# A down projection of seven quarter products by the Strassen-Winograd scheme, in a layer kernel whose order is planned

## The chip, the cores and the metric

One core of one Trainium2 chip. The metric is the device time of one execution in microseconds (us), as the median of several runs. A core has five engines that the text names: TensorE (PE; its weight loads, PEld, run beside the products), VectorE (DVE), ScalarE (ACT), GpSimd (POOL) and SyncE (SP), which here only issues transfers. They run side by side and wait for one another by semaphores. Products land in PSUM, of which the kernel has eight banks of 512 float32 columns on 128 partitions; everything else lies in SBUF.

## The reference

One layer of a diffusion backbone: 512 latent tokens and 256 context tokens of width 1024. A parallel attention and state-space mixer comes first, then a gated MLP. The change is in the last product of the MLP.

```python
D_MODEL, SEQ, D_FF, FFN_CONV = 1024, 512, 2816, 3

def conv_glu(h, w_up, conv_w, conv_b, w_down):
    gate, val = jnp.split(h @ w_up, 2, axis=-1)
    gate = depthwise_conv(gate, conv_w, conv_b)
    return (jax.nn.gelu(gate, approximate=False) * val) @ w_down
...
        ffn_x = conv_glu(modulate(rms_norm(x, ffn_pre_norm[l]), mod_x[3], mod_x[4]),
                         w_up[l], ffn_conv_w[l], ffn_conv_b[l], w_down[l])
        x = x + mod_x[5] * rms_norm(ffn_x, ffn_post_norm[l])
```

All arrays are float32.

## The kernel before

**Precision.** A product of float32 matrices is made of three products in the faster type F32R: `split` (L496 to 499) makes a high part by a copy on ACT (L498) and the rest, source minus high part, by a subtraction on DVE (L499). High times high, high times low and low times high are summed in PSUM. `weight` (L501) loads a block of weights and splits it; so each block of weights costs one transfer, one ACT copy and one DVE subtraction of its width.

**Stages, in order of time.** Input projections; state-space groups and attention, interleaved; the output projection (`natural_gemm`); the up projection; the down projection; the last norm and the output. The matmuls of the up projection are at L759 (in `gemm_T`, which several stages share), those of the down projection at L1519.

**Up.** For each of the 22 blocks j of 128 hidden columns, two blocks of weights, 1024 wide (`upw`), are multiplied with the normed tokens `h2`, into a pair of banks. That is 2 x 8 x 3 = 48 matmuls of 512 columns for a j. (The first three j, `EARLY`, go in two halves of 256 tokens.) `gated` (L1457) makes the convolution, the Gelu and the gate out of the two banks: one ACT operation (L1460), two DVE operations (L1461, L1463), ACT (L1465), DVE (L1466). The result, `gT[j]`, has 128 hidden columns on the partitions and 512 tokens in the row. `modblock(5, ...)` (L1300, its DVE operation at L587) and `modfinish` make the last gate row `g2` meanwhile.

**Down.** Two halves of 512 output columns, one after the other in the program, each with four banks, one for each 128 tokens. For each of 22 k, the half row of weights (256 KB) is loaded and split; in the first half `gT[k]` is split too (`parts`), and kept for the second. The last four k are kept back, and done one token block after another, so that a block is done early and its eviction lies beside the products of the next. The eviction takes the sum of squares on ACT (L1539) and multiplies with `g2` on DVE (L1540). When a token block has both halves, `last` (L1498) makes the norm's scale from the sums (L1503, L522 to 529), loads the rows held since the mixer, adds them (L1509), and stores.

**What sets the order.** Nothing above is executed in program order. The kernel is built twice: the first time to collect its instructions, then `plan` (L382) makes an order for each engine and a place for each buffer, and the second time the order is laid down by dependences. `price` (L162) gives a cost for each instruction; for a transfer it is a size divided by 360 (bytes by nanosecond), or `DMA_WORDS` for one that scatters words. `Graph.schedule` (L315) is a list scheduler over the five engines, which `best` runs forwards and backwards. SBUF is 212 units of 256 columns (`UNITS`), in blocks of four; a block holds one type at a time. `plan` gives each buffer a place that should be free by `MARGIN` (2500 ns) before the buffer's start in the last schedule, schedules again with the waits that the places bring, and repeats this `rounds` times. The round with the shortest time by these prices is used. `pins` are extra orders among matmuls: one kept group after another.

All loads and stores of the stages told of here are issued by SP, in one planned order. A transfer waits at the head of that queue until its buffer is free.

Of the kernel before, what the change touches and what calls it, by code (L numbers as in the profile page):

```python
# [11 lines left out]
F32 = mybir.dt.float32  # L12
# [138 lines left out]
AHEAD = 40000  # L151
DMA_START, DMA_WAIT, DMA_AHEAD, DMA_ALONE, DMA_WORDS = 650, 910, 3000, 0.8, 5000

# [8 lines left out]
def price(x):  # L162
# [6 lines left out]
    if "DMA" in kind:  # L169
        words = any(len(v.bass_ap.ap) > 1 and v.bass_ap.ap[-1][0] != 1 for v in x.outs if hasattr(v, "bass_ap"))  # L170
        return DMA_WORDS if words else size(ops[0]) * ops[0][1][0][1] * 4 / 360
    if e == "PE":
# [208 lines left out]

def plan(ins, pieces, hints, units, rounds=16):  # L382

# [20 lines left out]
    _, _, start, end = Graph(preds, eng, dma, cost, share, tables, urgent, opens, shared).best()  # L404
    found = None
    for _ in range(rounds):
        held, types = [(-1, -1e9, [])] * units, [None] * (units // 4)
        inst, before = [((), -1e9)] * (units // 4), [((), -1e9)] * (units // 4)
        full, places = [set(p) for p in preds], []
        for t, (n, type_), at in pieces:  # L410
# [10 lines left out]

            fit = [o for o in able if free[o] + MARGIN <= s0]
            fit = [o for o in fit if (o >= EDGE) == (n < 3)] or fit
# [20 lines left out]
        if found is None or took < found[0]:  # L444
            found = took, places, order
    return found
# [20 lines left out]
def build(nc, tc, ctx, a, out, dbg=None, places=None):  # L467
# [979 lines left out]

    gT = []
    EARLY = 3

    h2v = lambda k, p_: h2[k // 2 * 2 + p_][:, k % 2, :]
# [5 lines left out]
    def gated(j, gate, other, used):  # L1457

        cv = t2()
        act(cv, gate, AF.Identity, scale=R("fw", j * 3 + 1), bias=R("fb", j))  # L1460
        V.scalar_tensor_tensor(out=cv[:, 1:], in0=gate[:, : S - 1], scalar=R("fw", j * 3), in1=cv[:, 1:], op0=ALU.mult,  # L1461
                               op1=ALU.add)
        V.scalar_tensor_tensor(out=cv[:, : S - 1], in0=gate[:, 1:S], scalar=R("fw", j * 3 + 2), in1=cv[:, : S - 1],  # L1463
                               op0=ALU.mult, op1=ALU.add)
        act(cv, cv, AF.Gelu)  # L1465
        V.tensor_tensor(out=cv, in0=other, in1=cv, op=ALU.mult)  # L1466
        pfree(*used)
        gT.append(cv)


# [40 lines left out]

    lefts = {}
    for half in range(2):
        c0_ = half * 512
        po = [pget("a") for _ in range(NX)]

        def products(k, i, w, l):
            for lp, wp in ((0, 0), (0, 1), (1, 0)):
                mm(po[i], lhsT=l[lp][:, i * P : (i + 1) * P], rhs=w[wp], start=(k == 0 and lp == 0 and wp == 0),  # L1519
                   stop=(k == NF - 1 and lp == 1))  # L1520

        tail = []
        for k in range(NF):
            if not half:
                lefts[k] = parts(gT[k])
            w = weight(a["wdn"][k][:, c0_ : c0_ + 512], 512)
            if k < NF - 4:
                for i in range(NX):
                    products(k, i, w, lefts[k])
            else:  # L1530
                tail.append((k, w, lefts[k]))
        at = []
        for i in range(NX):
            began = here()
            for k, w, l in tail:
                products(k, i, w, l)
            at.append((began, here()))
            to = res[i][:, c0_ : c0_ + 512]
            act(t2(), po[i], AF.Square, accum_out=sums[i][:, half : half + 1])  # L1539
            V.tensor_tensor(out=to, in0=po[i], in1=g2[:, c0_ : c0_ + 512], op=ALU.mult)  # L1540
            pfree(po[i])
            if half:
                last(i, 2)
        pins.extend(zip(at, at[1:]))
    return sl.pieces, (pins, urgent, holds)

# [97 lines left out]
```

## Time and profile before

| what | us |
|---|---|
| median of 3 runs | 976.13 |
| lowest and highest | 975.1, 976.65 |
| the profiled execution | 976.79 |
| its span, from first to last instruction | 975.0 |

The profiled execution is one more execution; its span is 1.79 us shorter than its time, which also has what lies before the first and after the last instruction. The mean granted clock of TensorE in it is 0.995 of full speed.

The lines that follow in the prediction are of five kinds. The page's first part gives busy time, share and count of instructions of each engine; its second part cuts the span in 40 equal slices and gives tenths of busy time. A row of windows gives a stretch in us from the span's start, its length, then busy time and count for each engine, the granted clock, the share of the DMA engines and GB/s. A row of groups gives line, engine, operation, what is written and read, shapes, count, then busy time, mean ns of one, idle time of the engine before them and what ended it. A row of a line gives smallest, median and largest duration in ns and the first and last start. A row of the timeline, or of the chain of waits, gives start and length in us and what ran.

### The profile page before, as it was taken

To read this page: it belongs to the slowest core of one execution; us is meant where nothing else is said; L and a number is where in the kernel's file an instruction comes from. 1 tells how busy PE (TensorE), PEld (TensorE's weight loads), DVE (VectorE), ACT (ScalarE), POOL (GpSimd) and SP (SyncE) were. 2 spreads that over 40 slices of the span, in tenths; PEclk is the share of its full clock that TensorE was granted. 3 is DMA by queue.
4 is the path that set the end of the run, shared out by engine and by line. 5 is a ranking of instruction groups with operands and counts; after the bars stand their busy time and mean duration, and the time that the engine had idled before them with its cause. 6 is when DMAs were issued, how large, how long until landed. Compare 5 with 4: busy or idle time off the path is not lost.

```text
span 975.0 us, 14205 instructions
## 1 busy us (share of the span) xinstructions
PE 953.7 (98%) x5157; PEld 813.6 (83%) x5157; DVE 680.0 (70%) x1151; ACT 504.7 (52%) x1004; POOL 184.4 (19%) x187
## 2 busy tenths in 40 slices
PE   8999999999999999999899999999999999999997
PEld 7888888888878987888798888988888888878885
DVE  6999886999999987767789966735254342695214
ACT  4554337567579787787787026633142231662001
POOL 0002202657694535111010001000000000000000
PEclk9999999999999999999899999999999999999999
DMA  9924102012321351524839876231323203347321
GB/s 349 402 94 130 44 22 82 19 66 74 95 60 55 100 153 45 133 74 110 234 138 335 248 205 216 87 108 54 140 85 132 87 33 108 98 155 241 82 84 65
DMA packets 48037, 122.94 MB, mean 126 GB/s; under 512 B 8400, under 2 KB 11552, under 8 KB 47968
## 3 DMA queue, kind: packets, MB, share of 16 engines
q1 hardware_dynamic: 45424, 120.89, 38.6%
q10 hardware_dynamic: 2544, 1.15, 0.5%
q8 instruction: 41, 0.67, 0.3%
q14 instruction: 28, 0.23, 0.1%
HBM read 99.82 MB, written 6.46 MB: 109 GB/s over the span
## 4 chain that ended last, share of the span: by engine, by line
PE 80%; DVE 5%; DMA 3%; ACT 2%; issue 1%; POOL 0%; SPq 0%; DVEq 0%; ACTq 0%; POOLq 0%
PE banks L759 38%; PE banks L1519 12%; PE banks L1326 9%; PE banks L1203 5%; PE banks L1231 3%; PE banks L1219 3%; DVE block L499 2%; DMA block<-block 2%; PE banks L1135 1%; PE banks L686 1%; PE banks L1039 1%; PE banks L1084 1%; PE banks L1076 1%; DVE smalls L1205 1%; PE banks L808 1%
## 5 line engine op out<-in xcount | busy, mean ns | idle before, releaser
L759 PE MATMUL banks<-block,block 128*128 128x512 f32 (+1 forms) x2132 | 443.2, 360 | 1.1 <-DVE block L855 1.1
L759 PEld LDWEIGHTS banks<-block,block 128*128 128x128 f32 x2132 | 358.8, 188 | 62.1 <-DVE block L855 1.4
L499 DVE TENSOR_TENSOR block<-block,block 128x512 fp32r<-128x512 f32 (+4 forms) x252 | 221.7, 904 | 121.2 <-ACT block L498 59.2
L498 ACT ACTIVATE block<-block 128x512 fp32r<-128x512 f32 (+5 forms) x252 | 181.7, 746 | 220.6 <-PE banks L759 68.9
L1519 PE MATMUL banks<-block,block 128*128 128x512 f32 x504 | 118.1, 389 | 0.2 <-ACT block L498 0.2
L1519 PEld LDWEIGHTS banks<-block,block 128*128 128x128 f32 x504 | 94.4, 188 | 20.4 <-ACT block L498 0.8
L1203 PE MATMUL banks<-block,block 128*128 128x512 f32 (+1 forms) x384 | 97.8, 359 | 7.1 <-DMA block<-in_wout_dram 3.1
L522 POOL TENSOR_TENSOR smalls<-smalls,powers 128x1 f32<-128x1 f32 (+3 forms) x16 | 12.6, 789 | 482.5 <-DVE smalls L1503 355.4
L499 DVE TENSOR_TENSOR block<-banks,block 128x256 fp32r<-128x256 f32 (+1 forms) x156 | 84.1, 556 | 14.8 <-ACT block L498 13.8
L1326 PE MATMUL banks<-block,block 128*128 128x512 f32 x384 | 91.2, 393 | 0.0
L498 ACT ACTIVATE block<-banks 128x256 fp32r<-128x256 f32 (+1 forms) x156 | 74.8, 499 | 27.9 <-PE banks L1219 14.5
L1326 PEld LDWEIGHTS banks<-block,block 128*128 128x128 f32 x384 | 71.5, 188 | 14.3
L1203 PEld LDWEIGHTS banks<-block,block 128*128 128x128 f32 x384 | 61.0, 192 | 16.0 <-ACT block L1207 4.5
L1205 DVE TENSOR_REDUCE smalls<-banks 128x1 f32<-128x768 f32 x64 | 60.9, 951 | 17.5 <-PE banks L1203 13.8
L1231 PE MATMUL banks<-block,block 128*128 128x256 f32 x384 | 70.1, 297 | 0.0
L1207 ACT ACTIVATE block<-banks,smalls 128x768 f32<-128x768 f32 x64 | 57.9, 905 | 15.4 <-DVE smalls L1205 10.7
L1219 PE MATMUL banks<-cst,block 128*128 128x128 f32 x384 | 64.3, 275 | 0.2
L587 DVE SCALAR_TENSOR_TENSOR block<-block,block 128x1024 f32<-128x1024 f32 x50 | 60.0, 1217 | 3.8 <-DMA block<-in_wmod_dram 3.6
L1231 PEld LDWEIGHTS banks<-block,block 128*128 128x128 f32 x384 | 57.8, 191 | 4.5 <-issue 0.7
L793 DVE SCALAR_TENSOR_TENSOR block<-banks,cwh,block 128x510 f32<-128x510 f32 (+3 forms) x88 | 50.9, 619 | 8.1 <-ACT block L789 7.7
L1219 PEld LDWEIGHTS banks<-cst,block 128*128 128x128 f32 x384 | 47.3, 141 | 6.9 <-DVE block L499 0.8
L686 PE MATMUL banks<-block,block 128*128 128x512 f32 x192 | 48.3, 398 | 0.6 <-ACT block L640 0.6
(228 smaller groups left out, 980.1 us busy)
## 6 DMA issues: line engine op xcount, KB each, us to landing
block<-in_wmod_dram SPq DMA_DIRECT2D x48, 512.0 KB
block<-in_wup_dram SPq DMA_DIRECT2D x44, 512.0 KB
block<-in_wdn_dram SPq DMA_DIRECT2D x44, 256.0 KB
block<-block SPq DMA_DIRECT2D x32, 256.0 KB
block<-in_wout_dram SPq DMA_DIRECT2D x16, 512.0 KB
block<-block SPq DMA_DIRECT2D x56, 128.0 KB
block<-in_wxbc_dram SPq DMA_DIRECT2D x12, 512.0 KB
block<-in_wz_dram SPq DMA_DIRECT2D x16, 256.0 KB
```

Source lines behind the costliest of these rows:

```text
L498: act(hi, src, AF.Copy)
L499: (lo_eng or V).tensor_tensor(out=lo, in0=src, in1=hi, op=ALU.subtract)
L587: V.scalar_tensor_tensor(out=junk, in0=wt, scalar=0.5, in1=vec, op0=ALU.mult, op1=ALU.mult, accum_out=acc)
L686: mm(po[i], lhsT=hx[k][:, hp, i * P : (i + 1) * P], rhs=wz[wp], start=(k == 0 and wp == 0 and hp == 0), stop=(k == KD - 1 and hp == 1))
L759: mm(po, lhsT=wf(k, pt[0]), rhs=xf(k, pt[1]), start=(k == 0 and pt == parts[0]), stop=(k == nk - 1 and pt == parts[-1]))
L1203: mm(sc[:, o : o + n], lhsT=q_[:, x_, qi * P : (qi + 1) * P], rhs=kk[:, y_, :], start=part == 0, stop=part == 2)
L1205: V.reduce_max(nm, sc[:, :T], axis=AX.X, negate=True)
L1207: act(pe, sc[:, :T], AF.Exp, bias=nm, scale=1.0, accum_out=sm_)
L1219: nc.tensor.transpose((tx if c < NX else tc_)[:, o : o + P], pe[:, s_ : s_ + P], ident)
L1231: mm(po[:, half * 256 : half * 256 + 256], lhsT=vst(c), rhs=rhs, start=(part == 0 and c == 0), stop=(part == 1 and c == NKT - 1))
L1326: mm(po[i][:, nh * 512 : nh * 512 + 512], lhsT=l[lp][:, i * P : (i + 1) * P], rhs=w[wp][:, nh * 512 : nh * 512 + 512], start=(k == 0 and l ...
L1519: mm(po[i], lhsT=l[lp][:, i * P : (i + 1) * P], rhs=w[wp], start=(k == 0 and lp == 0 and wp == 0), stop=(k == NF - 1 and lp == 1))
```

## The change

The down projection is written as a product of two-by-two quarters. On the left, A is the activations: with tokens 0 to 255 and 256 to 511 as rows and hidden blocks 0 to 10 and 11 to 21 as columns, A11, A12 are the first tokens, A21, A22 the others. On the right, B has hidden blocks 0 to 10 and 11 to 21 as rows, and output columns 0 to 511 (`upper`) and 512 to 1023 (`lower`). In place of the eight quarter products there are seven, by Winograd's form of Strassen's scheme:

- sums of the left: A21 + A22, that minus A11, A11 - A21, and A12 minus the second (`mixed`). `combined` makes them on GpSimd in the up stage, four operations of 256 columns for each pair of hidden blocks (k, k + 11), as soon as block k + 11 is there. It also splits A11 and the first three sums, and keeps both parts of all four (`lefts[k]`, two buffers of 1024 columns).
- sums of the right: B12 - B11 (t1), B22 - t1 (t2_), B22 - B12 (t3), and B21 - t2_. They are made on DVE in the down stage.

The down stage is two series over the 11 pairs. Series 1 (`sums_of_right`) makes four products at once, two banks of 128 tokens for each: all eight banks. It loads a whole row of weights (512 KB) and half of another (256 KB), makes t1, t2_, t3, stores t2_ to DRAM, and splits B11, t2_, t3 and t1. Series 2 (`rest_of_right`) makes the other three, in six banks: it loads a whole row and t2_, makes B21 - t2_, splits it and both halves of the row, and splits `gT[11 + k]` and `mixed[k]`. A matmul is as before: 128x128 weights, 512 moving columns, three for each product of blocks. The last three (series 1) and four (series 2) pairs are kept back and done product by product. An eviction now adds a product to what was summed (`plus`), and where an output quarter is complete, `scaled` takes the squares on ACT and multiplies with `g2` on DVE.

Three things of the planner change: `DMA_WORDS` goes from 5000 to 10000; a transfer from SBUF to SBUF is priced at 180 in place of 360 bytes by nanosecond; and there are 56 rounds in place of 16, those from the tenth on with a margin drawn between 0 and 5000 ns, and every third of these starts again from the best schedule found.

```diff
@@ -149,7 +149,7 @@
          ("Pool", "Activation"): 75, ("Pool", "DVE"): 74, ("Pool", "PE"): 149, ("Pool", "Pool"): 102}
 
 AHEAD = 40000
-DMA_START, DMA_WAIT, DMA_AHEAD, DMA_ALONE, DMA_WORDS = 650, 910, 3000, 0.8, 5000
+DMA_START, DMA_WAIT, DMA_AHEAD, DMA_ALONE, DMA_WORDS = 650, 910, 3000, 0.8, 10000
 
 
 def engine_of(x):
@@ -168,7 +168,8 @@
     kind = type(x).__name__
     if "DMA" in kind:
         words = any(len(v.bass_ap.ap) > 1 and v.bass_ap.ap[-1][0] != 1 for v in x.outs if hasattr(v, "bass_ap"))
-        return DMA_WORDS if words else size(ops[0]) * ops[0][1][0][1] * 4 / 360
+        inside = all(isinstance(o[2].bass_ap.tensor, tile.Tile) for o in ops)
+        return DMA_WORDS if words else size(ops[0]) * ops[0][1][0][1] * 4 / (180 if inside else 360)
     if e == "PE":
         if ops[1][2].dtype == mybir.dt.float32r:
             return size(ops[1]) / (2.4 if size(ops[1]) >= 256 else 1.2) + (13 if ops[1][1][0][1] > 64 else 100)
@@ -379,7 +380,7 @@
         return found
 
 
-def plan(ins, pieces, hints, units, rounds=16):
+def plan(ins, pieces, hints, units, rounds=56):
 
 
 
@@ -402,8 +403,10 @@
                     preds[i].update(last)
     opens, shared = {u[0] for u in users.values()}, [ports(x) for x in ins]
     _, _, start, end = Graph(preds, eng, dma, cost, share, tables, urgent, opens, shared).best()
-    found = None
-    for _ in range(rounds):
+    found, rng = None, np.random.default_rng(0)
+    for n_ in range(rounds):
+        if n_ > 8 and n_ % 3 == 0:
+            start, end = kept_
         held, types = [(-1, -1e9, [])] * units, [None] * (units // 4)
         inst, before = [((), -1e9)] * (units // 4), [((), -1e9)] * (units // 4)
         full, places = [set(p) for p in preds], []
@@ -419,7 +422,7 @@
                         able.append(o)
                         free[o], due[o] = max(max(v[1] for v in h), (before if types[b] == type_ else inst)[b][1]), h
 
-            fit = [o for o in able if free[o] + MARGIN <= s0]
+            fit = [o for o in able if free[o] + (MARGIN if n_ < 9 else rng.uniform(0, 2 * MARGIN)) <= s0]
             fit = [o for o in fit if (o >= EDGE) == (n < 3)] or fit
             if fit:
                 o = max(fit, key=lambda o: sum(v[1] for v in due[o]) / len(due[o]))
@@ -442,7 +445,7 @@
             continue
         took, order, start, end = Graph(full, eng, dma, cost, share, tables, urgent, opens, shared).best()
         if found is None or took < found[0]:
-            found = took, places, order
+            found, kept_ = (took, places, order), (start, end)
     return found
 
 
@@ -1445,8 +1448,24 @@
                  ahead=lambda n: transposes(*tails[n]))
 
 
-    gT = []
+    gT, mixed, lefts = [], {}, {}
     EARLY = 3
+    HF = NF // 2
+
+    def combined(j):
+
+        if j < HF:
+            return
+        k = j - HF
+        a11, a21, a12, a22 = gT[k][:, :256], gT[k][:, 256:], gT[j][:, :256], gT[j][:, 256:]
+        s_, mixed[k] = t4(P, 3, 256), t2(P, 256)
+        G.tensor_tensor(out=s_[:, 2], in0=a11, in1=a21, op=ALU.subtract)
+        G.tensor_tensor(out=s_[:, 0], in0=a21, in1=a22, op=ALU.add)
+        G.tensor_tensor(out=s_[:, 1], in0=s_[:, 0], in1=a11, op=ALU.subtract)
+        G.tensor_tensor(out=mixed[k], in0=a12, in1=s_[:, 1], op=ALU.subtract)
+        lefts[k] = [t4(P, 4, 256, dt=F32R) for _ in range(2)]
+        split(lefts[k][0][:, 0], lefts[k][1][:, 0], a11)
+        split(lefts[k][0][:, 1:], lefts[k][1][:, 1:], s_)
 
     h2v = lambda k, p_: h2[k // 2 * 2 + p_][:, k % 2, :]
 
@@ -1466,6 +1485,7 @@
         V.tensor_tensor(out=cv, in0=other, in1=cv, op=ALU.mult)
         pfree(*used)
         gT.append(cv)
+        combined(j)
 
 
     upw = lambda j: [weight(a["wup"][2 * j + s_]) for s_ in range(2)]
@@ -1509,39 +1529,98 @@
             V.scalar_tensor_tensor(out=res[i][:, h], in0=res[i][:, h], scalar=c0, in1=xr[:, h], op0=ALU.mult, op1=ALU.add)
             load(out[i * P : (i + 1) * P, h], res[i][:, h])
 
-    lefts = {}
-    for half in range(2):
-        c0_ = half * 512
-        po = [pget("a") for _ in range(NX)]
-
-        def products(k, i, w, l):
-            for lp, wp in ((0, 0), (0, 1), (1, 0)):
-                mm(po[i], lhsT=l[lp][:, i * P : (i + 1) * P], rhs=w[wp], start=(k == 0 and lp == 0 and wp == 0),
-                   stop=(k == NF - 1 and lp == 1))
+    tsum = nc.dram_tensor("weight_sums", (HF, P, 512), F32, kind="Internal").ap()
+    upper, lower = slice(0, 512), slice(512, 1024)
+
+    def term(po, l, w, i, first, stop):
+        for lp, wp in ((0, 0), (0, 1), (1, 0)):
+            mm(po, lhsT=l[lp][:, i * P : (i + 1) * P], rhs=w[wp], start=first and lp == 0 and wp == 0, stop=stop and lp == 1)
+
+    def parted(src):
+        w = t2(dt=F32R), t2(dt=F32R)
+        split(*w, src)
+        return w
+
+    def sums_of_right(k):
+
+        raw, b22 = t4(), t2()
+        load(raw, a["wdn"][k])
+        load(b22, a["wdn"][HF + k][:, 512:])
+        b11, b12 = raw[:, upper], raw[:, lower]
+        t1, t2_, t3 = t2(), t2(), t2()
+        V.tensor_tensor(out=t1, in0=b12, in1=b11, op=ALU.subtract)
+        V.tensor_tensor(out=t2_, in0=b22, in1=t1, op=ALU.subtract)
+        V.tensor_tensor(out=t3, in0=b22, in1=b12, op=ALU.subtract)
+        load(tsum[k], t2_)
+        l = lambda n: [lefts[k][p_][:, n] for p_ in range(2)]
+        return (l(0), parted(b11)), (l(2), parted(t2_)), (l(3), parted(t3)), (l(1), parted(t1))
+
+    def rest_of_right(k):
+
+        raw, t2_ = t4(), t2()
+        load(raw, a["wdn"][HF + k])
+        load(t2_, tsum[k])
+        V.tensor_tensor(out=t2_, in0=raw[:, upper], in1=t2_, op=ALU.subtract)
+        hi, lo = t4(P, 3, 256, dt=F32R), t4(P, 3, 256, dt=F32R)
+        split(hi[:, :2], lo[:, :2], gT[HF + k].rearrange("p (a b) -> p a b", a=2))
+        split(hi[:, 2], lo[:, 2], mixed[k])
+        l = lambda n: [hi[:, n], lo[:, n]]
+        return (l(1), parted(t2_)), (l(2), parted(raw[:, lower])), (l(0), parted(raw[:, upper]))
+
+    def series(terms, banks, keep, done, order):
 
         tail = []
-        for k in range(NF):
-            if not half:
-                lefts[k] = parts(gT[k])
-            w = weight(a["wdn"][k][:, c0_ : c0_ + 512], 512)
-            if k < NF - 4:
-                for i in range(NX):
-                    products(k, i, w, lefts[k])
+        for k in range(HF):
+            now = terms(k)
+            if k < HF - keep:
+                for (l, w), po in zip(now, banks):
+                    for i in range(2):
+                        term(po[i], l, w, i, k == 0, False)
             else:
-                tail.append((k, w, lefts[k]))
+                tail.append((k, now))
         at = []
-        for i in range(NX):
+        for n, i in order:
             began = here()
-            for k, w, l in tail:
-                products(k, i, w, l)
+            for k, now in tail:
+                term(banks[n][i], *now[n], i, k == 0, k == HF - 1)
             at.append((began, here()))
-            to = res[i][:, c0_ : c0_ + 512]
-            act(t2(), po[i], AF.Square, accum_out=sums[i][:, half : half + 1])
-            V.tensor_tensor(out=to, in0=po[i], in1=g2[:, c0_ : c0_ + 512], op=ALU.mult)
-            pfree(po[i])
-            if half:
-                last(i, 2)
+            done(n, i, banks[n][i])
+            pfree(banks[n][i])
         pins.extend(zip(at, at[1:]))
+
+    p1, u2, u3 = ([t2() for _ in range(2)] for _ in range(3))
+
+    def scaled(src, i, half):
+        act(t2(), src, AF.Square, accum_out=sums[i][:, half : half + 1])
+        o = half * 512
+        V.tensor_tensor(out=res[i][:, o : o + 512], in0=src, in1=g2[:, o : o + 512], op=ALU.mult)
+
+    plus = lambda to, po, other: V.tensor_tensor(out=to, in0=po, in1=other, op=ALU.add)
+
+    def summed_first(n, i, po):
+        if n == 0:
+            act(p1[i], po, AF.Copy)
+        elif n == 1:
+            plus(u2[i], po, p1[i])
+        elif n == 2:
+            plus(u3[i], po, u2[i])
+        else:
+            plus(u2[i], po, u2[i])
+            to = t2()
+            plus(to, po, u3[i])
+            scaled(to, 2 + i, 1)
+
+    banks = lambda n: [[pget("a") for _ in range(2)] for _ in range(n)]
+    series(sums_of_right, banks(4), 3, summed_first, [(n, i) for n in range(4) for i in range(2)])
+
+    def summed_last(n, i, po):
+        to, at = t2(), (2 + i, i, i)[n]
+        plus(to, po, (u3, u2, p1)[n][i])
+        scaled(to, at, (0, 1, 0)[n])
+        if n != 1:
+            last(at, 2)
+
+    series(rest_of_right, banks(3), 4, summed_last, [(n, i) for n in range(3) for i in range(2)])
     return sl.pieces, (pins, urgent, holds)
 
 
```

## The prediction

> **What bounds the kernel now.** First the page: its span, the busy shares, and the slices of TensorE and VectorE.
>
> ```profile
> span 975.0 us, 14205 instructions
> PE 953.7 (98%) x5157; PEld 813.6 (83%) x5157; DVE 680.0 (70%) x1151; ACT 504.7 (52%) x1004; POOL 184.4 (19%) x187
> ...
> PE   8999999999999999999899999999999999999997
> ...
> DVE  6999886999999987767789966735254342695214
> ```
>
> TensorE (PE) is busy in every slice. The reader is to see two halves: up to slice 23 VectorE (DVE) is nearly as full, after that it is half empty. A busy PE isn't proof of a PE bound, so the second view is the windows by stage (us; busy time and count of PE, weight loads, DVE, ACT, POOL; granted clock; DMA).
>
> ```profile
> 10.00:65.00 55.00, 52.23 (x303) 45.26 (x302) 49.15 (x108) 29.76 (x49) 2.66 (x2) 1.00 0.81 312
> 65.00:155.00 90.00, 89.80 (x475) 75.97 (x474) 77.11 (x137) 39.91 (x62) 10.32 (x13) 1.00 0.24 76
> 155.00:270.00 115.00, 113.47 (x659) 97.63 (x659) 103.34 (x162) 74.24 (x176) 73.24 (x62) 1.00 0.22 61
> 270.00:390.00 120.00, 116.07 (x692) 97.54 (x692) 105.71 (x183) 98.43 (x247) 65.87 (x65) 1.00 0.31 83
> 390.00:520.00 130.00, 125.36 (x861) 112.77 (x860) 103.28 (x177) 103.51 (x226) 20.04 (x21) 0.97 0.51 147
> ...
> 780.00:848.00 68.00, 68.00 (x302) 56.33 (x301) 27.16 (x38) 23.32 (x38) 0.00 (x0) 1.00 0.24 78
> 848.00:968.00 120.00, 119.81 (x529) 98.60 (x527) 55.86 (x100) 32.01 (x60) 1.66 (x3) 1.00 0.39 127
> 968.00:975.00 7.00, 0.31 (x2) 0.00 (x0) 3.28 (x8) 1.04 (x4) 0.55 (x1) 0.86 0.23 86
> ```
>
> The last stage but one, 848 to 968, is the down projection: 119.81 of 120 us PE at full clock, while DVE has 64 us free and ACT 88. The up stage before it (780 to 848) has no PE gap at all. So here a matmul fewer is time less, as long as what feeds it stays beside it. The third view, line 1519 alone in the same window, and its forms:
>
> ```profile
> 848.00:968.00 120.00, 119.74 (x528) 98.42 (x526) 1.00 0.39 127
> ```
> ```profile
> L1519 PE MATMUL banks<-block,block x504: 388/389/497, 847.7 to 967.9; 128*128 128x512 f32 x168
> L1519 PE MATMUL banks<-block x24: 389/389/389, 876.6 to 959.1; 128*128 128x512 f32 x24
> ```
>
> The counts agree with the code: 2 halves x 22 rows of weights x 3 products of high and low parts x 4 token blocks = 528. One matmul costs 119.74 / 528 = 0.2268 us from start to start; the 389 ns of a single one is latency, pipelined.
>
> **Matmuls removed.** Seven quarter products: 7 x 11 pairs of rows x 3 x 2 token blocks = 462, same shape and same 512 moving columns. 66 fewer: 66 x 0.2268 = **-15.0 us**. This is the only large term, and it sits on an unbroken PE.
>
> **VectorE work added in the down stage.** All prices are from these rows: the splits of 512 columns in this window (mean of one), and four and ten of them queued.
>
> ```profile
> L499 DVE TENSOR_TENSOR block<-block,block 128x512 fp32r<-128x512 f32 x53 | 33.9, 685 | 27.0 <-PE banks L1519 16.3 <-ACT block L498 9.2 <-issue 1.3
> L587 DVE SCALAR_TENSOR_TENSOR block<-block,block 128x1024 f32<-128x1024 f32 x8 | 9.7, 1224 | 3.8 <-DMA block<-in_wmod_dram 3.6
> ```
> ```profile
> 852.71 2.48 DVE L499 TENSOR_TENSOR block<-block,block 128x512 fp32r<-128x512 f32 x4
> 855.71 6.28 DVE L499 TENSOR_TENSOR block<-block,block 128x512 fp32r<-128x512 f32 x10
> ```
>
> Queued, one follows the other after (2.48 - 0.685) / 3 = 0.60 or (6.28 - 0.685) / 9 = 0.62 us. Now the list. Series 1, per pair k: three sums of weights and four splits, 7 operations; PE takes 24 matmuls = 5.44 us, DVE 7 x 0.62 = 4.3. Series 2: the difference t2_, three splits of weights, one of the left operand, and one of 256 columns (0.36, an estimate: a bit over half); PE 18 matmuls = 4.08 us, DVE 3.5. Evictions of series 1: DVE does n=1, 2 (two each) and n=3 (three for each of two): 10. So before PE reaches the last products of series 2 (72 matmuls kept back, so 390 x 0.2268 = 88.5 us after the start) DVE must have done 77 + 10 + 11 + 11 + 25 (the kept four pairs need only their first weight by then) = 134 operations of 512 and 11 of 256: 134 x 0.60 + 4 = 84 us at best, 134 x 0.685 + 4 = 96 us at worst. **DVE goes from half empty to level with PE.** Ends for the stall that this adds: 0 (a head start in the up stage, and 64 free us become used) and 96 - 88.5 = 7.5 us. I take +2.0, nearer to the queued rows, since this work is queued and its order isn't forced to wait for PE. One thing presses on it: the eight 1224 ns operations of line 587 (modblock of source 5, 9.8 us) now run in the down window; their result g2 is wanted by the n=3 evictions of series 1, so they come earlier or crowd series 1. ACT gets 4 copies per pair in series 1 and 5 in series 2, about 11 x 9 x 0.6 = 59 us of 105: no bound.
>
> **The up stage.** From step 11 on each step adds four GpSimd operations of 256 columns and splits of 256 and 768 columns on ACT and DVE. The nearest rows, GpSimd 128x256 (min/median/max) and DVE splits while GpSimd works (155 to 520 us):
>
> ```profile
> L1064 POOL TENSOR_TENSOR block<-block x32: 727/741/1713, 188.7 to 373.0; 128x256 f32<-128x256 f32 x32
> ```
> ```profile
> L499 DVE TENSOR_TENSOR block<-banks,block 128x512 fp32r<-128x512 f32 x82 | 55.5, 683 | 9.1 <-ACT block L498 8.5
> L499 DVE TENSOR_TENSOR block<-block,block 128x512 fp32r<-128x512 f32 x51 | 44.0, 874 | 1.3 <-ACT block L498 1.2
> ```
>
> GpSimd: 4 x 0.74 = 3.0 us per step, on an engine with nothing to do there. DVE: 0.40 of a step now (27.16 / 68), that is 4.4 of 48 x 0.2268 = 10.9 us, plus some 1.4 us of new splits. PE stays the bound: cost 0; if that cover were gone it would be PE waiting for weight splits, which I bound by 0 and 2 us over the stage. What GpSimd does to DVE shows in the rows: 874 ns against 685 for the same split from SBUF, and no loss where the source is in PSUM (683). The Trainium skill, "SBUF — State Buffer", section "Who interferes with whom", has the rule: a DVE instruction with two SBUF inputs and a GpSimd instruction that reads SBUF exclude one another. The trace agrees (874 against 685 against 683). By that rule alone 44 new GpSimd operations would bar up to 44 x 0.74 = 33 us of DVE's time in the 120 us of steps 11 to 21 and leave 2 us per step, not 5, for a head start; that would press the DVE-bound rival below. Nothing in the sum is taken from it.
>
> **Start of series 1.** It takes all eight banks, where half 0 took four. The last step's eviction now runs from 848.99 (ACT) to 855.79:
>
> ```profile
> 848.99 0.78 ACT L1460 ACTIVATE block<-banks,prm 128x512 f32<-128x512 f32 x1
> ...
> 855.11 0.68 DVE L1466 TENSOR_TENSOR block<-banks,block 128x512 f32<-128x512 f32 x1
> ```
>
> That is 6.8 us, in which n=3 has no bank. Pair 0's n=0 to 2 (18 matmuls, 4.1 us) cover part, pair 1 the rest if it is ready, and early pairs may run inside the last up steps. Time to prepare two pairs is there: row 780:848 leaves DVE 41 us. Space is the doubt: of 212 units, 32 (h2), 88 (lefts, when complete), 22 + 11 (gT, mixed), 4 (g2) and up to 24 (weights of a step) are held, which leaves 31, and a pair needs 28 while it is made and 16 until used; a second fits early only where the last lefts (8 a pair) aren't made yet. Bounds 0 and 6.8 - 4.1 = 2.7 us; I take +0.5.
>
> **The end.** Now, the chain of waits:
>
> ```profile
> 967.73 0.70 ACT block L1539 x2
> 968.43 0.02 issue
> 968.45 0.69 DVE block L1540
> ```
>
> Afterwards a DVE sum (0.69) stands before the Square (0.6), where now a second Square of 0.6 delays it. Cost +0.1 by these rows; if the one operation queues behind the previous block's two of line 1509, up to +1.0. I take +0.3.
>
> **DMA.** Down weights go in whole rows: 512 + 256 KB in and 256 KB out per pair in series 1, 768 KB in series 2, so 1 MB per 5.44 us, about 190 GB/s, against 312 GB/s in the window from 10 to 65. Hidden, at 0, if the issue order is good; the bad order is the slower rival.
>
> **The search.** It plans the whole kernel anew, with other DMA prices. Outside the last two stages PE stands still for 2.8 + 0.2 + 1.5 + 3.9 + 4.6 = 13 us from 10 to 520 us. The largest stall, in 10 us windows (PE alone):
>
> ```profile
> 470.00:480.00 10.00, 9.40 (x76) 1.00 1.02 302
> 480.00:490.00 10.00, 7.45 (x34) 0.66 0.71 211
> ```
>
> DMA is saturated, PE waits 2.6 us, and the clock falls to 0.66, which costs up to 10 x 0.34 = 3 us more. Copies from SBUF to SBUF now get twice the price, so this stall may go, and others may come. Bounds -7 and +7 (half of 13, either way); I take -1.0. The Trainium skill, "TensorE: Matmul & The Clock Gate", Part 1, says an idle window of about 3.4 us halves the clock until a busy one; here 2.6 us of idle went with 0.66. By that rule a single long wait in the down stage costs more than its length, while the same sum in short ones doesn't; rival one would then be dearer by 2 to 3 us.
>
> **Sum.** The profiled execution took 976.79 us (span 975.0, 1.79 around it), 0.66 above the median 976.13. The terms are differences, so I put them on the median: 976.13 - 15.0 + 2.0 + 0.5 + 0.3 - 1.0 = **962.9 us**.
>
> **Rivals.**
> - *DVE becomes the bound* of the down stage: at 685 ns each, or with the modblocks left inside, the stall is 7.5 us, not 2: 976.13 - 15.0 + 7.5 + 0.5 + 0.3 = 969, up to 974. For it: 84 to 96 us of work against 88.5. Against: DVE at 103 of 115 us (155 to 270) leaves PE 113.5.
> - *The search finds more*: the 470 to 490 stall goes with its slow clock, -6 in place of -1, and DVE hides: 955 to 957.
> - *Slower: buffers serialise the weights.* Place: loads on SP, which issues in order, behind a store of t2_ or a slot still in use. Price by the chain's one wait for this tensor:
>
> ```profile
> 858.61 3.93 DMA block<-in_wdn_dram
> ```
>
>   If a pair's load can start only when the last pair's splits are done, its period is 3.9 + 4.3 = 8.2 us against 5.44: 2.8 lost per pair, 31 over series 1, so 976 - 15 + 31 = 992. It decides from the sixth such pair (15 / 2.8). For it: operands hold 125 units all through series 1. Against: 87 are left, three pairs of 28, and the lefts free 8 per pair.
> - That the change doesn't do what it says is nearly excluded: 462 follows from the loops.
>
> **Chances.** Forecast (959 to 967) 0.55; DVE bound (967 to 974, its end no change) 0.21; search 0.16; serialised 0.08. The range 955 to 972 leaves out the lower end of the search case (0.05), the upper of the DVE case (0.06) and the slower one: 0.19. A measurement tells about 0.2% (2 us) from no change: faster 0.89, same 0.03, slower 0.08.
>
> **What would show it.** 462 matmuls in the down stage at 0.227 us; PE gaps there of 2 to 3 us in total, ended by ACT or DVE line 499; DVE near 90% there; GpSimd some 33 us in the up stage with no PE gap; an end of 7 to 8 us. Gaps ended by DMA, or a clock under 1.00 after 614 us, would show the slower case; PE idle from 10 to 520 far from 13 us, the search.

## The result, and the profile after

The changed kernel takes 965.84 us (median of 4 runs, 964.26 to 967.57), the kernel before 976.39 in the same comparison: ratio 0.9894, 95% interval 0.9871 to 0.9917, faster by 10.6 us. 962.9 was forecast, in a range from 955 to 972.

The page of the changed kernel, with the lines that answer to those of before:

```profile
span 965.2 us, 14340 instructions
PE 942.7 (98%) x5091; PEld 800.1 (83%) x5091; DVE 754.0 (78%) x1264; ACT 535.5 (55%) x1061; POOL 228.7 (24%) x231
...
PE   7999999999999999999999999999999999999995
...
DVE  5999966997989997668899985754254755499997
```

PE has 66 instructions less, and VectorE, half empty at the end of the kernel before, now stands at 9 in the last slices. The windows of the last stages, and the matmuls of the down projection (now at line 1537):

```profile
780.00:835.00 55.00, 55.00 (x245) 45.53 (x244) 26.21 (x34) 12.98 (x20) 17.70 (x19) 1.00 0.21 66
...
840.00:860.00 20.00, 20.00 (x90) 16.52 (x89) 18.15 (x26) 10.04 (x17) 12.71 (x13) 1.00 0.54 162
860.00:880.00 20.00, 19.74 (x85) 15.24 (x84) 20.00 (x31) 8.47 (x15) 4.07 (x4) 1.00 0.64 207
880.00:900.00 20.00, 20.00 (x90) 16.48 (x89) 20.00 (x33) 14.43 (x27) 0.00 (x0) 1.00 0.69 218
...
835.00:950.00 115.00, 114.74 (x503) 93.76 (x502) 107.29 (x174) 64.75 (x120) 17.32 (x17) 1.00 0.57 185
950.00:966.00 16.00, 4.31 (x20) 3.22 (x18) 10.85 (x27) 2.76 (x8) 2.08 (x3) 0.72 0.28 104
```
```profile
L1537 PE MATMUL banks<-block,block x462: 388/389/505, 848.1 to 953.9; 128*128 128x512 f32 x154
```

Three numbers cut the span in stages, for this kernel and for every run below: the start of the first down matmul, the start of the last, and the span. These are of the profiled execution; the time is the median of each run. The kernel before took 977.05 us in the comparison of e1 to e3, 977.73 in that of e4 to e7 and 976.86 in that of e8 and e9, and the ratios below are against these.

| run | time, us | first down matmul | last | from first to last | end (span less last) | span |
|---|---|---|---|---|---|---|
| before | 976.39 | 847.7 | 967.9 | 120.2 | 7.1 | 975.0 |
| changed | 965.84 | 848.1 | 953.9 | 105.8 | 11.3 | 965.2 |
| e1 kept products in order | 955.33 | 838.0 | 943.5 | 105.5 | 9.6 | 953.1 |
| e2 search alone | 970.72 | 839.6 | 960.0 | 120.4 | 7.4 | 967.4 |
| e3 products alone | 965.70 | 847.8 | 953.9 | 106.1 | 9.0 | 962.9 |
| e4 plan of changed, kept in order | 962.82 | 845.5 | 951.5 | 106.0 | 9.0 | 960.5 |
| e5 plan of e1, kept side by side | 955.54 | 837.3 | 943.9 | 106.6 | 9.7 | 953.6 |
| e6 changed, another draw | 958.63 | 837.5 | 944.9 | 107.4 | 10.9 | 955.8 |
| e7 more VectorE work | 967.35 | 841.7 | 951.2 | 109.5 | 14.0 | 965.2 |
| e8 control for e4 | 966.73 | 848.4 | 954.3 | 105.9 | 11.6 | 965.9 |
| e9 as e1, another draw | 958.27 | 838.8 | 947.3 | 108.5 | 9.0 | 956.3 |

Read along the first two rows, the gain of 9.8 us of span is -14.4 in the down matmuls, +4.2 at the end, and +0.4 ahead of them. The first is what the change is about. The other two are what the experiments are for: why the end grew, and why a longer search brought nothing ahead of it.

What happens at the end, in the timeline of the changed kernel (start, length, engine, line; the last matmul starts at 953.9):

```profile
951.18 1.29 DVE L1598 TENSOR_TENSOR block<-banks,block 128x512 f32<-128x512 f32 x2 [2.55 <-PE banks L1537]
...
952.98 1.28 DVE L1598 TENSOR_TENSOR block<-banks,block 128x512 f32<-128x512 f32 x2
...
954.35 0.69 DVE L1598 TENSOR_TENSOR block<-banks,block 128x512 f32<-128x512 f32 x1
...
956.93 0.74 DVE L1529 SCALAR_TENSOR_TENSOR block<-block,smalls,block 128x512 f32<-128x512 f32 x1
...
957.67 1.41 DVE L1529 SCALAR_TENSOR_TENSOR block<-block,smalls,block 128x512 f32<-128x512 f32 x2
958.99 0.69 DVE L1596 TENSOR_TENSOR block<-block,block 128x512 f32<-128x512 f32 x1
959.59 0.75 DVE L1529 SCALAR_TENSOR_TENSOR block<-block,smalls,block 128x512 f32<-128x512 f32 x1
960.25 0.69 DVE L1596 TENSOR_TENSOR block<-block,block 128x512 f32<-128x512 f32 x1
960.85 1.41 DVE L1529 SCALAR_TENSOR_TENSOR block<-block,smalls,block 128x512 f32<-128x512 f32 x2
```

VectorE waits 2.55 us for PE; then five sums with banks (L1598) come within 3.9 us around the last matmul, and from 956.93 to 962.26 VectorE is busy with products by the gate row (L1596) and with the adds of `last` (L1529) for three token blocks. The planned order of matmuls shows why so many come at once. Only the order within a series is laid down. The last product of series 1 has 32 of its 33 matmuls done by number 339 of 462; the one that is left stands at number 450, between the ends of the last two products of series 2 (448 and 462). Three of the five sums hang on it: the two that this product needs, and that of a product of series 2, complete at number 428, which is added to the first of these two. The kernel before finished its two halves side by side too, there matmul by matmul, with the ends of a token block two to four matmuls apart: two Squares, of two halves, follow one another after each wait for PE.

```profile
962.46 0.60 ACT L1539 ACTIVATE block<-banks 128x512 f32<-128x512 f32 x1 [9.74 <-PE banks L1519]
...
963.05 0.59 ACT L1539 ACTIVATE block<-banks 128x512 f32<-128x512 f32 x1
```

### The profile page after: what moved, and what is told of

Read it like the earlier page. It is cut to its first block, busy times and chain, and to the rows that moved or that the text cites. A ratio compares the mean times of both kernels' runs of the same rounds, so it can differ in the third digit from the quotient of the medians.

```text
span 965.2 us, 14340 instructions
## 1 busy us (share of the span) xinstructions
PE 942.7 (98%) x5091; PEld 800.1 (83%) x5091; DVE 754.0 (78%) x1264; ACT 535.5 (55%) x1061; POOL 228.7 (24%) x231
## 3 DMA queue, kind: packets, MB, share of 16 engines
q10 hardware_dynamic: 2544, 1.15, 0.4%
## 4 chain that ended last, share of the span: by engine, by line
PE 83%; DVE 7%; ACT 3%; issue 3%; DMA 3%; POOL 1%; SPq 0%; DVEq 0%; POOLq 0%; ACTq 0%
PE banks L762 41%; PE banks L1537 9%; PE banks L1329 8%; PE banks L1206 5%; PE banks L689 5%; PE banks L1234 3%; PE banks L1222 3%; DVE block L502 3%; PE banks L1138 2%; PE banks L1042 1%; PE banks L1087 1%; PE banks L600 1%; DVE smalls L1208 1%; DMA block<-block 1%; ACT block L501 1%
## 5 line engine op out<-in xcount | busy, mean ns | idle before, releaser
L762 PEld LDWEIGHTS banks<-block,block 128*128 128x128 f32 x2132 | 359.9, 189 | 63.1 <-DVE block L502 2.8
L501 ACT ACTIVATE block<-block 128x512 fp32r<-128x512 f32 (+5 forms) x307 | 209.3, 716 | 162.3 <-PE banks L762 31.8
L502 DVE TENSOR_TENSOR block<-block,block 128x512 fp32r<-128x512 f32 (+5 forms) x307 | 259.4, 877 | 46.4 <-PE banks L762 19.7
L1537 PE MATMUL banks<-block,block 128*128 128x512 f32 x462 | 106.0, 390 | 0.3 <-DVE block L502 0.2
L1537 PEld LDWEIGHTS banks<-block,block 128*128 128x128 f32 x462 | 86.3, 188 | 19.7 <-DVE block L502 1.7
L1329 PE MATMUL banks<-block,block 128*128 128x512 f32 x384 | 91.3, 392 | 0.0
L1329 PEld LDWEIGHTS banks<-block,block 128*128 128x128 f32 x384 | 71.4, 188 | 14.1
L1208 DVE TENSOR_REDUCE smalls<-banks 128x1 f32<-128x768 f32 x64 | 60.9, 952 | 11.3 <-PE banks L1206 7.4
L1206 PEld LDWEIGHTS banks<-block,block 128*128 128x128 f32 x384 | 60.8, 189 | 8.9 <-ACT block L1210 3.4
L1234 PEld LDWEIGHTS banks<-block,block 128*128 128x128 f32 x384 | 57.1, 189 | 4.6 <-ACT block L501 1.1
L1480 DVE SCALAR_TENSOR_TENSOR block<-banks,prm,block 128x511 f32<-128x511 f32 x22 | 16.3, 748 | 54.7 <-ACT block L1479 54.7
L1462 POOL TENSOR_TENSOR block<-block 128x256 f32<-128x256 f32 x11 | 10.9, 995 | 197.7 <-PE banks L762 179.8
```

Source lines behind the costliest of these rows:

```text
L501: act(hi, src, AF.Copy)
L502: (lo_eng or V).tensor_tensor(out=lo, in0=src, in1=hi, op=ALU.subtract)
L762: mm(po, lhsT=wf(k, pt[0]), rhs=xf(k, pt[1]), start=(k == 0 and pt == parts[0]), stop=(k == nk - 1 and pt == parts[-1]))
L1206: mm(sc[:, o : o + n], lhsT=q_[:, x_, qi * P : (qi + 1) * P], rhs=kk[:, y_, :], start=part == 0, stop=part == 2)
L1208: V.reduce_max(nm, sc[:, :T], axis=AX.X, negate=True)
L1234: mm(po[:, half * 256 : half * 256 + 256], lhsT=vst(c), rhs=rhs, start=(part == 0 and c == 0), stop=(part == 1 and c == NKT - 1))
```

## The experiments

Two theories were set against one another. **Pile-up:** the long end comes from products of both series being finished side by side. **Search:** the plan of everything ahead of the down stage is a draw, worth several us either way, and this kernel drew a poor one.

### One part at a time

e1 adds one order among matmuls to the changed kernel; everything is planned anew:

```diff
-    series(sums_of_right, banks(4), 3, ...)
+    kept1 = series(sums_of_right, banks(4), 3, ...)
...
-    series(rest_of_right, banks(3), 4, ...)
+    kept2 = series(rest_of_right, banks(3), 4, ...)
+    pins.append((kept1[-1], kept2[0]))
```

> One more order among matmuls: the kept products of series 2 only after those of series 1; everything is planned anew. Pile-up theory (the changed kernel runs both series' kept products side by side at the end, so the evictions of both series queue on VectorE behind the last matmul, 11 us from the last matmul to the end of the span): the end falls to 7 or 8 us, the down matmuls keep 106 us from first to last start, and the time is 961 to 963 us. Rival (VectorE is full in this stage anyway and its work only moves forward): the end falls, but gaps of 3 us or more ended by VectorE appear among the down matmuls, and the time stays at 965 to 968 us. An order elsewhere that comes out otherwise can shift either by 2 us; read the stages, not the total alone.

955.33 us, ratio 0.9778 (0.9751 to 0.9806): below what either theory gave. The table shows where: the end falls by 1.7 us only, and the start of the down stage comes 10.1 us sooner, in a part of the kernel that the edit doesn't touch.

e2 is the kernel before with the changed planner (`rounds=56`, drawn margins, both new transfer prices), e3 the changed kernel with the planner of before.

> The kernel before with the planner of the changed kernel (56 rounds, other margins, other transfer prices); the eight products stay. If the search is worth nothing by itself, as the equal start of the down stage in both traces says (847.7 and 848.1 us): 975 to 977 us. Rival (the search is worth some 4 to 6 us, and the products less than they seem): 970 to 972 us.

> The changed kernel with the planner of before (16 rounds, old prices). If the seven products carry the gain: 964 to 968 us, with the down matmuls at 106 us and an end above 9 us where both series' kept products run side by side. Rival (without the longer search the plan finds no place for the sums and operands): 970 us or more, with gaps in the down or the up stage.

e2 takes 970.72 us, ratio 0.9933 (0.991 to 0.9955): its rival holds, and its first down matmul stands at 839.6, where before and e3 have 847.7 and 847.8. e3 takes 965.7 us, ratio 0.9883 (0.986 to 0.9905), with 106.1 us of down matmuls: the seven products carry a gain of 11.4 us (977.05 for before in this comparison, less 965.70) without the longer search, which alone gives 6.3. Together that would be nearly 18 us; the changed kernel shows 10.6. So something was lost in it, if the two gains add, and the starts of the down stage (848.1, and 839.6 in e2) put it ahead of that stage. The end of e3 is 9.0 us, where more than 9 was expected with the series side by side: its plan completes series 1 by matmul 380 of 462.

### The same plan ahead, a different end, and the other way round

e4 and e5 keep each engine's order for all instructions ahead of the down stage, and all places of buffers, and schedule only the rest anew. e4 takes the plan of the changed kernel and adds the order of e1, e5 takes the plan of e1 and takes that order away.

```diff
+    chain = {(i, j) for o in order.values() for i, j in zip([i for i in o if i < cut], [i for i in o if i < cut][1:])}
...
+    for i, before in kept:
+        preds[i].update(before)               # e4; e5: difference_update
...
+    took, order, _, _ = min(g.best(), g.schedule(kept_[0], 0.0), key=lambda s: s[0])
```

> The changed kernel with every engine's order up to the down stage and all places of buffers as they are, and only the down stage scheduled anew, with series 2's kept products after those of series 1. Pile-up theory (the end is long because both series' kept products finish together): first down matmul at 848 us as before, 106 us of down matmuls, the end falls from 11 to 8 or 9 us, time 962 to 964 us. Rival (the kept order is worth nothing by itself; the 10 us between the changed kernel and the one with kept order are a luckier plan of the attention stage): the end stays at 10 us or more, or gaps take what it gives; time 964.5 to 967 us.

> The plan of the first run (kept in order), orders up to the down stage and places frozen, and the down stage scheduled anew without the kept order, so that series 2's kept products may run beside series 1's. If the 10 us of the first run come from the part ahead of the down stage: first down matmul again at 838 us, an end of 10 to 12 us, time 955 to 958 us. If they come from the kept order: the time goes back to 963 us or more.

e4 has an end of 9.0 us, from 11.3; its time, 962.82 us, ratio 0.9866 (0.9846 to 0.9885), is within what pile-up gave. But its first down matmul comes at 845.5, not at 848 as expected, so more than half of its 4.7 us of span isn't the end's; that is taken up below. e5 takes 955.54 us, as e1: first down matmul at 837.3, an end of 9.7. So the 10 us between the changed kernel and e1 lie in the plan ahead of the down stage. The kept order isn't what brought them, and with that plan it isn't even needed for a shorter end: series 1 is complete by matmul 328 in e5 as in e1.

e6 is the changed kernel with `default_rng(2)` in place of `default_rng(0)`. e7 adds a sum of no use to each pair:

```diff
+        V.tensor_tensor(out=t2(), in0=b22, in1=b11, op=ALU.subtract)
...
+        V.tensor_tensor(out=t2(), in0=raw[:, upper], in1=raw[:, lower], op=ALU.subtract)
```

> The changed kernel with other random margins in the search, nothing else. If the result of the search ahead of the down stage is a draw of several us: the first down matmul starts anywhere from 838 to 848 us, and not within 1 us of 848; down matmuls again 106 us from first to last, whatever the draw. If the plan isn't sensitive to the draw: first down matmul at 847 to 849 us, time 964 to 967 us.

> The changed kernel with one more sum of 512 columns on VectorE, of no use, for each pair in each series: 22 x 0.6 = 13 us more VectorE work in the down stage; planned anew. If VectorE is at its limit there (107 of 115 us busy): first to last down matmul goes from 106 to 111 us or more, with gaps ended by VectorE. If there is still cover (7 us free in the stage, 28 in the last up steps): 106 to 108 us.

e6 takes 958.63 us, ratio 0.9817 (0.9797 to 0.9836), 7 us under the changed kernel, by another row of random margins alone. The gain is again ahead of the down matmuls. These take 107.4 us, not the 106 expected: PE stands still for 1.45 us between 835 and 860 us, waiting for splits on ScalarE and VectorE.

e7 takes 967.35 us, ratio 0.9908 (0.9892 to 0.9924); 109.5 us from first to last down matmul, 3.7 more than in the changed kernel, and an end of 14.0. Of the 13 us that were added, 6.4 come out as time of these two stages. This is a new draw too: the other plans of the seven products take 115.0 to 118.3 us for both stages together and e7 takes 123.5, so against them it is 5.2 to 8.5. VectorE has 2 us left in the window:

```profile
835.00:950.00 115.00, 113.49 (x496) 92.44 (x495) 113.08 (x184) 61.96 (x118) 19.25 (x19) 1.00 0.57 183
```

That lies between the two expectations: there was cover for about half, and none for the other half. The end of 14.0 isn't a pile-up of the two series, since this plan completes series 1 by matmul 302.

### A control, and one more draw

e8 is e4 without the kept order. e9 is e1 with `default_rng(5)`.

> Control for the fourth run: the changed kernel, orders up to the down stage and places frozen, the down stage scheduled anew in the same way, but without the kept order. If the kept order shortens the end: an end of 10.5 us or more here against 9.0 us there, and a time 1.5 to 2.5 us above it, 964 to 966 us. If the shorter end there came from scheduling anew alone: 9 us, 962.5 to 963.5 us. The first down matmul stands at 848 us if TensorE's clock falls between 220 and 230 us as in the profile of the changed kernel, and at 845.5 us if it doesn't.

> The first run (kept in order) with other random margins. If the plan ahead of the down stage is a draw: its first down matmul stands anywhere from 836 to 848 us, with 106 us of down matmuls and an end of 9 to 10 us, so the time is its start plus 117 us (953 to 967 us). If the kept order brings the early start: 838 us within 1 us and 954 to 957 us.

e8 has an end of 11.6 us where e4 has 9.0, with the same order ahead: 2.6 us is what the kept order is worth in this plan, in the profiled executions. The wait of VectorE for PE is there again in e8: 3.54 us, ahead of a sum with a bank at 951.83.

The medians lie 3.9 us apart (966.73 and 962.82; 964 to 966 was expected for e8), the lowest runs only 0.45 (962.80 and 962.35), and the ratios' intervals, 0.9858 to 0.9907 and 0.9846 to 0.9885, overlap. Among executions with a mean clock of 0.994 or more, the spans are 961.0 and 961.8 us in e8 and 960.4 to 961.6 in e4, 0.6 apart in the mean. The worth of the kept order in time is therefore not settled closer than that.

Over all runs, the end goes with the place of series 1's last matmul. In the changed kernel, e8 and e6 it is number 450, 453 and 448 of 462, VectorE waits 2.5 to 3.5 us for PE just before, and the end is 10.9 to 11.6 us. In e1, e3, e4, e5 and e9 it is number 380 or earlier, no wait of VectorE for PE there is over 0.6 us, and the end is 9.0 to 9.7 us, with the order laid down or without it.

e9 takes 958.27 us, ratio 0.9812 (0.9792 to 0.9832), first down matmul at 838.8. It doesn't tell its two theories apart: the start is the early one, the time is not. Its down matmuls take 108.5 us, not the 106 expected.

### What the changed kernel's plan lost

Its order ahead of the down stage, run in e4, brings the first down matmul at 845.5; in the profiles of the changed kernel and of e8 it comes at 848.1 and 848.4. The granted clock tells them apart (in e8, 0.82 and 0.50 in the same windows). Two windows of the changed kernel (PE alone, clock behind the count):

```profile
220.00:225.00 5.00, 3.85 (x26) 0.81 0.76 252
225.00:230.00 5.00, 5.00 (x13) 0.51 0.00 1
```

and of e4:

```profile
220.00:225.00 5.00, 3.85 (x29) 1.00 0.68 247
225.00:230.00 5.00, 3.88 (x21) 1.00 0.12 31
```

The timeline there, of the changed kernel, and then of e4, which has the same order:

```profile
219.51 1.90 PE L1087 MATMUL banks<-block,block 128*128 128x64 f32 x16
222.56 2.20 PE L848 MATMUL banks<-ones,block 128*128 128x1 f32 x12 [1.15 <-ACT block L818]
...
225.20 3.62 PE L762 MATMUL banks<-block,block 128*128 128x512 f32 x8
```
```profile
219.14 1.90 PE L1106 MATMUL banks<-block,block 128*128 128x64 f32 x16
222.18 1.47 PE L867 MATMUL banks<-ones,block 128*128 128x1 f32 x12 [1.15 <-ACT block L837]
...
223.83 1.98 PE L781 MATMUL banks<-block,block 128*128 128x512 f32 x8
```

The same eight matmuls of 512 columns take 3.62 and 1.98 us. Ahead of them stand 5 us of matmuls of 64 and of 1 column with a wait of 1.15 us. The matmul behind them starts at 228.61 and 225.65, 2.96 us apart, where the narrow ones were 0.37 apart; that is 2.6 us lost.

It doesn't seem to happen in every execution: the spans of e8 are 961.0 and 961.8 with a mean clock of 0.994 and 0.995, and 964.2 to 965.9 with 0.988 to 0.992; those of the changed kernel are 962.4 (0.994), 962.9 and 965.2 (both 0.992) and 965.8 (0.988). The mean doesn't say where the clock fell, and some profiles, that of e8 among them (0.66), show another fall between 10 and 20 us. So this order costs some 2.6 us where the fall comes, and how often it comes is open.

That the clock's fall is what makes the difference follows from the two profiles; that the narrow matmuls set it off was only argued, since no run changes them. In e7 the clock falls to 0.69 between 220 and 225 us, behind the same twelve matmuls of one column, with no wait of PE at all.

The rest is the draw itself: without that fall, 845.5 against 837 to 842 with the five other plans that the new planner made (e1 and e5, e2, e6, e7, e9). The attention stage shows a part of it, in the windows of the changed kernel and then of e1 (those of before are in the prediction):

```profile
155.00:270.00 115.00, 113.85 (x642) 97.32 (x642) 98.08 (x156) 73.00 (x169) 68.82 (x58) 0.97 0.20 60
270.00:390.00 120.00, 116.54 (x677) 95.68 (x676) 106.11 (x183) 97.98 (x246) 72.17 (x69) 1.00 0.35 93
390.00:520.00 130.00, 129.06 (x899) 115.68 (x899) 106.89 (x181) 107.82 (x234) 19.94 (x21) 1.00 0.56 168
```
```profile
155.00:270.00 115.00, 114.76 (x658) 97.97 (x657) 103.89 (x162) 74.06 (x174) 69.57 (x59) 1.00 0.25 71
270.00:390.00 120.00, 117.92 (x725) 100.74 (x723) 109.51 (x189) 100.30 (x251) 70.53 (x69) 1.00 0.34 89
390.00:520.00 130.00, 129.43 (x883) 115.82 (x882) 110.46 (x182) 112.05 (x235) 20.85 (x21) 1.00 0.58 173
```

PE stands still in these 365 us for 10.1 us in the kernel before, 5.6 in the changed kernel and 2.9 in e1, where the clock stays at 1.00. Between 10 and 65 us it is 4.2 in the changed kernel and 1.9 in e1. With the 2.6 us of the clock that leaves some 3 of the 10.1 us between the changed kernel and e1 that no PE gap in these windows shows.

## Why the prediction was right, and which steps were off

The time, 965.84 us, lies in the range and 2.9 us above the forecast. By its steps:

- **Matmuls removed, -15.0.** Right: 462 of the same shape. From first to last start they take 105.8 us, where 461 x 0.2268 = 104.6 would be an unbroken row of them. So 1.2 us were given back; the kernel before had 0.7 of its own (120.2 less 527 x 0.2268), and -14.4 came through.
- **VectorE, +2.0.** Right in kind, and smaller: as a difference to the kernel before it is 1.2 less 0.7, some +0.5. VectorE is level with PE (20.00 of 20 us busy from 860 to 880 and from 880 to 900), and nearly all of the loss lies in the first of these windows (85 matmuls, where the others have 90), in waits for the subtraction of a split. e7 shows how little cover was left: of 13 us more, about half came out as time. The DVE-bound rival was that near.
- **Start of series 1, +0.5.** It cost nothing that shows here: PE has no gap from 835 to 860 us. In e6 and e9 it did, 1.45 and 1.1 us in that window.
- **Up stage, 0.** Right: 55.00 of 55 us PE. GpSimd was mis-sized: 44 us more on the page, not 33. The first of the four operations, which reads one buffer, as the row did that priced it, keeps its median; the last, which reads two, takes 1.6 times as long. The second reads two as well and has a median of 855 ns, and the shortest of each takes 737 to 740, so the second buffer alone doesn't make the difference; whether VectorE's own operations, which the prediction named as a bar, do was not tried.

```profile
L1462 POOL TENSOR_TENSOR block<-block x11: 739/744/1723, 753.5 to 858.3; 128x256 f32<-128x256 f32 x11
...
L1465 POOL TENSOR_TENSOR block<-block,block x11: 737/1182/1712, 756.4 to 862.9; 128x256 f32<-128x256 f32 x11
```

- **The end, +0.3 (at most +1.0).** This step failed: +4.2. It counted one DVE sum before the last Square, as if the last product alone stood behind the last matmul. The runs show that the plan finishes the last product of series 1 beside the last two of series 2, and that five sums and the last steps of three token blocks then queue on an engine that was just made full. That products without an order between them can be finished side by side could have been read in the profile before: its Squares came in pairs. Where series 1 is complete in time (e4 and four others) the end is still 9.0 to 9.7, so about 2 of the 4 us are the pile-up. Of the rest, 1.1 us are VectorE working on two blocks at once: in e4 the last sum starts at 953.00, 1.1 us after the last matmul's end (951.5 + 0.39), behind an add of the block before. The last 0.8 us were not taken apart.

```profile
952.33 0.75 DVE L1549 SCALAR_TENSOR_TENSOR block<-block,smalls,block 128x512 f32<-128x512 f32 x1
953.00 0.68 DVE L1619 TENSOR_TENSOR block<-banks,block 128x512 f32<-128x512 f32 x1
953.60 0.74 DVE L1549 SCALAR_TENSOR_TENSOR block<-block,smalls,block 128x512 f32<-128x512 f32 x1
```

- **The search, -1.0 (-7 to +7).** It gave +0.4 here, for two opposite reasons: the wait of 2.6 us at 480 is gone, as was thought possible, and another fall of the clock came at 220. As a term it was under-sized: the five other plans by the new planner start the down stage 6 to 10 us sooner than before. The rival "the search finds more" was true of the search, not of this draw.
- **The rivals.** Serialised weights did not come: no gap there is ended by DMA, at 185 GB/s. The time that agrees hides errors of 3.9 (end) and 1.4 us (search) one way, and of 1.4 (down stage: -13.0 with its stall, measured -14.4) and 0.5 (its start) the other; that so much of it cancels is luck.

On the clock the prediction named a section of the Trainium skill, "TensorE: Matmul & The Clock Gate", Part 1: an idle window of about 3.4 us halves the clock. The trace agrees with the half (0.51). It shows no idle window of that length: the longest wait there is 1.15 us, and whether the matmuls of one column behind it count as idle no run here shows.

The fastest of all versions are e1 and e5, at 955.33 and 955.54 us, with one plan ahead of the down stage: about 22 us under the kernel before in their comparisons.

## What to carry to other kernels

Where a profile shows one engine without a gap beside one that is half empty, trading matmuls for sums pays nearly in full, but only until the second engine is level; work out its whole list up to the last matmul, and expect the difference in what is queued at the end. Where an order is planned for the whole program, each edit redraws all of it: compare stage by stage, freeze the rest, or make several draws, before a difference is put down to the edit. Two kept-back groups with no order between them may be finished together, as in three of the six plans here, and then so are their evictions.

## What the runs showed of the hardware

TensorE's clock fell to about half (0.81 and 0.51 in two windows of 5 us) with no wait longer than 1.15 us, after 5 us of matmuls of 64 columns and of one. In e8, with the same order, it fell again (0.82 and 0.50); in e4, with the same order too, it stayed at 1.00.
